# A two-block transformer with a mixture of experts on one core: a reordered router, and expert tiles placed in other buffers

## The chip, the cores and the metric

The kernel runs on one core of a Trainium2 chip. The metric is the device time of one execution, in microseconds, with the weights in HBM at the start and the result written back to HBM.

## The reference, cut to what matters

256 tokens of width 1024 in float32 pass two blocks. The first block (a recurrent and pooling mixer, cross attention, a convolutional feed-forward layer, a conformer convolution, cross attention, the feed-forward layer again) is touched by the change only in which buffers its tiles take. The second block:

```python
def second_block(x, g_mix, w_in, sinks, w_br_dil, w_br_swa, w_out, g_ffn, w_group, b_group,
                 w_router, b_router, w_e_gate, w_e_up, w_e_down, g_final):
    h = rmsnorm(x, g_mix)
    q_d, k_d, v_d, q_s, k_s, v_s, gate_d, gate_s = split_cols(h @ w_in, IN_WIDTHS)
    y_dil = dilated_attention(q_d, k_d, v_d)          # 3 groups of 8 heads
    y_swa = swa_sink_attention(q_s, k_s, v_s, sinks)  # 16 heads, 2 of keys and values
    mixed = sigmoid(gate_d) * (y_dil @ w_br_dil) + sigmoid(gate_s) * (y_swa @ w_br_swa)
    x = x + mixed @ w_out
    x = x + hier_moe(rmsnorm(x, g_ffn), w_group, b_group, w_router, b_router,
                     w_e_gate, w_e_up, w_e_down)
    return rmsnorm(x, g_final)

def hier_moe(h, ...):
    g_logits = h @ w_group + b_group                  # 4 groups, the best one is taken
    e_logits = (h @ w_router + b_router)              # 8 experts of that group, the best two
    ...
    for e in range(32):
        a = silu(h @ w_e_gate[e]) * (h @ w_e_up[e])   # 1024 -> 512
        out = out + gates[:, e:e + 1] * (a @ w_e_down[e])
    return out
```

## The kernel before, in words

Every projection but the experts' is done as three fast matmuls on a split of both sides: ACT makes the high half of a weight tile (`whl`, L219), DVE the low half (L220), and x is held as xth and xtl. Weights come through SP's DMA queue into a ring of three 1 MiB buffers. SP, PE, DVE, ACT and POOL each run their own instructions in program order; a tile framework sets the waits and hands out buffers, and `after` (L325) adds an order without a wait.

**End of the second attention.** `block2_attn` takes its activations from one ring of 16 buffers, `p4`. `proj_rows` multiplies `mixed` by the four w_out tiles; the last two are gone through by quarters of the result (`b` = 0 to 3: token half, column half), and after each quarter the `Norm` class adds the residual to x on DVE (L67), makes xn = x times the gain g_ffn (L73), sums squares on ACT (L84), transposes xn on PE (L354) into PSUM, from where ACT copies it to xnT (L356).

**The router.** `moe` (from L1128) loads the group's and the router's weights as one tile wr of 1024 x 36 (L1155, ACT's queue). `logits` keeps wr as the stationary side, so the result lp lies as 36 x 128; ACT copies it (L1172) and PE transposes it back (L1186). DVE then scales by the token's norm and adds the biases (L1191), picks group and experts (`first_max`, L1120 to 1125), and a matmul with a triangle counts each expert's tokens (L1213). Each expert has 32 slots, four experts (a quad) fill the 128 rows of PE. `gather` (L1238) multiplies xn with a 0/1 matrix and so brings a quad's tokens into slots, 4 chunks of 128 columns at a time.

**The experts.** Eight quads; for each, 8 streams of 1 MiB of gate weights (G), 8 of up weights (U), 8 of down weights (Y, in two halves), 192 MiB in all. One stream is four matmuls (L1325), one for each expert. The tiles live wherever there is room: `wl` counts the streams and takes buffers in a fixed rotation of 22 units of 1 MiB: pairs (2 MiB tiles, L1297) and single homes (L1285). A home in a buffer of the attention (ring, split buffers, xth, xtl, rows, x itself) is issued as soon as SP comes to it and its buffer is free. SP's queue is in order.

x is added to the output accumulators in PSUM by four residual matmuls (L1275), after which x's own buffer is a home. `turn` scales G and U by the gate and transposes them; `scatter` (L1361) brings a half of Y back to the tokens. After the last scatter, ACT squares the four accumulator quarters (L342), DVE and POOL make the norm, and DVE multiplies by it and by the final gain gf (L1408), which was broadcast to all partitions by a DMA.

The rotation before:

```python
pairs = two(r2a[0], "w2") * NR2A + two(r2b, "w3") * NR2B        # 3 and 2 pairs
homes = [lambda s: whole(r2a[1], "w4", s)]
homes += [lambda s: whole(self.ring, "w", s)] * 3
homes += [lambda s: whole(self.spl[0], "whl", s)] * 4
homes += [lambda s: halves([half(self.rows, "row") for _ in range(2)], s)]
homes += [lambda s: whole(self.xtp, "xth", s), lambda s: whole(self.xtp, "xtl", s)]
homes += [lambda s: whole(self.xp, "x", s)]
```

Of the kernel before, what the change touches and what calls it, by code (L numbers as in the profile page):

```python
# [16 lines left out]
P = 128  # L17
# [8 lines left out]
NR2A = 3  # L26
NR2B = 2
# [4 lines left out]
class FM:  # L32


    def __init__(self, k, n, dt, name):
        self.t = [k.b4([P, min(4, n - i), T], dt, f"{name}{i}") for i in range(0, n, 4)]
# [7 lines left out]
class Norm:  # L44
# [57 lines left out]
    def stats(self, t):  # L102
# [3 lines left out]
        nc.vector.scalar_tensor_tensor(r, ss[:, t, 0:1], EPS, ss[:, t, 1:2], op0=OP.add, op1=OP.add)  # L106
# [33 lines left out]

class Kern:
    def __init__(self, ctx, tc, a, out):
        self.tc, self.nc, self.a, self.out = tc, tc.nc, a, out
        self.uid = self.nspl = 0
# [16 lines left out]
    def b4(self, shape, dt=F32, name="b4"):  # L161
        return self.p4.tile(shape, dt, tag="b4", name=self.nm(name))
# [113 lines left out]
    def proj_tm(self, acc, w, ah, al, first):  # L276
# [4 lines left out]
        for k in range(2):  # L281
            for t in range(2):
                sh = ah(k)[:, t * P:(t + 1) * P]
                sl = al(k)[:, t * P:(t + 1) * P]
                st = first and k == 0
                for h in range(2):
                    nc.tensor.matmul(acc[t][h], sh, wh(k)[:, h * 512:(h + 1) * 512], start=st, stop=False)  # L287
                for h in range(2):
                    nc.tensor.matmul(acc[t][h], sh, wl(k)[:, h * 512:(h + 1) * 512], start=False, stop=False)  # L289
                for h in range(2):  # L290
                    nc.tensor.matmul(acc[t][h], sl, wh(k)[:, h * 512:(h + 1) * 512], start=False, stop=False)

    def proj_rows(self, acc, w, ah, al, order, first=True, last=True, norm=None):
# [11 lines left out]
        for b in range(4):  # L305
            t, h = divmod(b, 2)
            ts_ = slice(t * P, (t + 1) * P)
            hs = slice(h * 512, (h + 1) * 512)
            for j, (i, wh, wl) in enumerate(ws):
# [591 lines left out]
    def block2_attn(self, norm):  # L901
# [20 lines left out]
        def qproj(n0, nch, sc0, name):  # L922
            q = FM(self, nch, F32, name)
# [30 lines left out]
        ysh = FM(self, 8, F32R, "ysh")  # L954
        ysl = FM(self, 8, F32R, "ysl")
        qd, kd, vd = [], [], []

        def dil_proj(g):

            q_ = FM(self, 4, F32, "qd")  # L960
            k_ = FM(self, 4, F32, "kd")
            v_ = self.b4([P, 2, 512], F32, "vd")
# [112 lines left out]
        for g in range(3):  # L1075
            steps += dil_proj(g)
        self.reserve(ysh, ysl)
# [5 lines left out]
        ydh = FM(self, 4, F32R, "ydh")  # L1083
        ydl = FM(self, 4, F32R, "ydl")
        gd = FM(self, 8, F32, "gd")
        gs = FM(self, 8, F32, "gs")
# [41 lines left out]
    def moe(self, ctx, m, r2a):  # L1128
# [3 lines left out]
        y2 = pool("y2", 2)  # L1132
# [5 lines left out]

        def t2(shape, name, dt=F32):
            return y2.tile(shape, dt, tag="y2", name=self.nm(name))  # L1140
# [20 lines left out]
        lt = m1([36, 2, P], F32, "lt")  # L1161
# [443 lines left out]
```

## Time and profile before

| | |
|---|---|
| median of 3 runs | 1627.76 us (1627.60 to 1628.19) |
| profiled execution | 1636.39 us |
| its span | 1634.5 us |
| mean granted PE clock | 0.951 of full speed |
| PE, DVE, ACT, POOL busy | 91%, 52%, 41%, 5% |
| HBM read | 393.94 MB, 242 GB/s over the span |

A share of busy time is a mean over a program whose parts differ. Up to about 1150 us PE is busy nine tenths of the time and the DMA engines half of it; from about 1195 us to the end the experts' weights stream, the DMA engines are busy all the time and PE seven tenths. So a change near 1150 to 1200 us is read from windows there and from the queue that issues the weights, not from the shares of the whole. In the timelines a row gives its start, its length, engine, line and operation; in brackets stands the idle time before it and what ended it. Starts are those of the one profiled execution, in us from its span's start.

### The profile page before, as it was taken

To read this page: it belongs to the slowest core of one execution; us is meant where nothing else is said; L and a number is where in the kernel's file an instruction comes from. 1 tells how busy PE (TensorE), PEld (TensorE's weight loads), DVE (VectorE), ACT (ScalarE), POOL (GpSimd) and SP (SyncE) were. 2 spreads that over 40 slices of the span, in tenths; PEclk is the share of its full clock that TensorE was granted. 3 is DMA by queue.
4 is the path that set the end of the run, shared out by engine and by line. 5 is a ranking of instruction groups with operands and counts; after the bars stand their busy time and mean duration, and the time that the engine had idled before them with its cause. 6 is when DMAs were issued, how large, how long until landed. Compare 5 with 4: busy or idle time off the path is not lost. (4 is left out here: it accounts for less than half of the span.)

```text
span 1634.5 us, 23715 instructions
## 1 busy us (share of the span) xinstructions
PE 1479.8 (91%) x9724; PEld 1133.7 (69%) x9724; DVE 851.4 (52%) x1553; ACT 663.8 (41%) x1061; POOL 82.4 (5%) x146
## 2 busy tenths in 40 slices
PE   8999999999989999999999999999998777676665
PEld 7988889999987688999988789789643222221211
DVE  7975677666899566776676765765500000000000
ACT  5764555545676454545554444454311000000001
POOL 0000000000057000100000000000000000000000
PEclk9999999999999999999999999999989878897887
DMA  7555445555643443655545236247999999999996
GB/s 265 193 188 180 143 167 191 185 192 187 218 151 104 161 162 104 219 181 194 186 162 206 99 128 213 78 153 286 356 381 423 421 423 425 424 422 421 425 423 268
DMA packets 52049, 396.58 MB, mean 243 GB/s; under 512 B 5952, under 2 KB 6112, under 8 KB 12256
## 3 DMA queue, kind: packets, MB, share of 16 engines
q1 hardware_dynamic: 49824, 388.80, 62.0%
q0 software_dynamic: 1680, 5.79, 1.1%
q8 instruction: 78, 1.28, 0.3%
q10 hardware_dynamic: 432, 0.41, 0.1%
q14 instruction: 35, 0.29, 0.0%
HBM read 393.94 MB, written 1.05 MB: 242 GB/s over the span
## 5 line engine op out<-in xcount | busy, mean ns | idle before, releaser
L220 DVE TENSOR_TENSOR whl<-w,whl 128x1024 fp32r<-128x1024 f32 (+1 forms) x344 | 404.8, 1184 | 207.3 <-ACT whl L219 206.7
L219 ACT ACTIVATE whl<-w 128x1024 fp32r<-128x1024 f32 (+1 forms) x344 | 345.7, 1020 | 296.3 <-PE pr L270 147.0
L267 PE MATMUL pr<-xth,whl 128*128 128x256 f32 x1472 | 370.0, 283 | 0.0
L268 PE MATMUL pr<-xtl,whl 128*128 128x256 f32 x1472 | 366.8, 281 | 0.0
L267 PEld LDWEIGHTS pr<-xth,whl 128*128 128x128 f32 x1472 | 277.3, 188 | 3.7 <-issue 2.8
L268 PEld LDWEIGHTS pr<-xtl,whl 128*128 128x128 f32 x1472 | 277.2, 188 | 1.9 <-issue 1.1
L270 PE MATMUL pr<-xth,whl 128*128 128x256 f32 x1472 | 236.7, 281 | 1.2 <-DVE whl L220 1.2
L270 PEld LDWEIGHTS pr<-xth,whl 128*128 128x128 f32 x1472 | 200.4, 188 | 2.9 <-issue 1.5
L1387 DVE TENSOR_TENSOR as<-sg,tp 128x512 f32<-128x512 f32 x8 | 5.5, 687 | 241.1 <-ACT GUs L1330 117.2
L1325 PE MATMUL U<-w,xq 128*32 128x512 f32 x512 | 81.0, 719 | 37.4 <-DMA w<-in_w_e_dram 37.3
L1325 PE MATMUL Y<-w,as 128*32 128x512 f32 x512 | 77.4, 737 | 30.4 <-DMA w<-in_w_e_dram 25.4
L1325 PE MATMUL G<-w,xq 128*32 128x512 f32 x512 | 74.0, 671 | 32.5 <-DMA w<-in_w_e_dram 32.5
L1349 DVE COPY sct<-st 128x256 f32<-128x256 f32 x8 | 3.4, 424 | 160.9 <-PE st L1347 160.9
L1325 PEld LDWEIGHTS Y<-w,as 128*32 128x32 f32 x512 | 16.0, 126 | 84.0 <-DMA w<-in_w_e_dram 39.0
L1325 PEld LDWEIGHTS U<-w,xq 128*32 128x32 f32 x512 | 14.4, 119 | 84.0 <-DMA w<-in_w_e_dram 49.7
L1325 PEld LDWEIGHTS G<-w,xq 128*32 128x32 f32 x512 | 13.4, 116 | 83.3 <-DMA w<-in_w_e_dram 62.4
L1395 ACT ACTIVATE ys<-Y,sm 128x512 f32<-128x512 f32 x16 | 11.0, 687 | 130.0 <-PE Y L1325 130.0
L1330 ACT ACTIVATE GUs<-G,sm 128x512 f32<-128x512 f32 x8 | 5.5, 687 | 129.1 <-PE G L1325 129.1
L827 DVE SCALAR_TENSOR_TENSOR cps<-gl,vec,cps 128x252 f32<-128x252 f32 (+18 forms) x144 | 56.1, 468 | 1.7 <-ACT cps L797 1.6
L819 POOL TENSOR_TENSOR cv<-cv,prod 128x470 f32<-128x470 f32 (+9 forms) x40 | 50.4, 1263 | 18.8 <-ACT prod L815 16.3
L287 PE MATMUL pa<-whl,ah 128*128 128x512 f32 x160 | 49.4, 390 | 0.0
L289 PE MATMUL pa<-whl,ah 128*128 128x512 f32 x160 | 49.4, 390 | 0.0
(438 smaller groups left out, 2318.7 us busy)
## 6 DMA issues: line engine op xcount, KB each, us to landing
w<-in_w_e_dram SPq DMA_DIRECT2D x94, 1024.0 KB, 22.5
w<-in_w_e_dram SPq DMA_DIRECT2D x45, 2048.0 KB, 22.3
w<-in_f_w_up_dram SPq DMA_DIRECT2D x48, 1024.0 KB, 4.8
w<-in_w_in_dram SPq DMA_DIRECT2D x25, 1024.0 KB, 4.8
w<-in_f_w_down_dram SPq DMA_DIRECT2D x24, 1024.0 KB, 4.9
w<-in_c_w_pw_dram SPq DMA_DIRECT2D x12, 1024.0 KB, 4.9
w<-in_ab_w_in_dram SPq DMA_DIRECT2D x9, 1024.0 KB, 5.0
w<-in_xa_wk_dram SPq DMA_DIRECT2D x8, 1024.0 KB, 4.9
```

Source lines behind the costliest of these rows:

```text
L219: c = self.last_hi = nc.scalar.activation(h[:, s], src[:, s], AF.Copy)
L220: d = nc.vector.tensor_sub(l[:, s], src[:, s], h[:, s].bitcast(F32))
L267: nc.tensor.matmul(ps[:, j], wh(k)[:, js], xh(k), start=(k == 0), stop=False)
L268: nc.tensor.matmul(ps[:, j], wh(k)[:, js], xl(k), start=False, stop=False)
L270: nc.tensor.matmul(ps[:, j], wl(k)[:, js], xh(k), start=False, stop=(k == kc - 1))
L287: nc.tensor.matmul(acc[t][h], sh, wh(k)[:, h * 512:(h + 1) * 512], start=st, stop=False)
L289: nc.tensor.matmul(acc[t][h], sh, wl(k)[:, h * 512:(h + 1) * 512], start=False, stop=False)
L819: nc.gpsimd.tensor_add(y, y, pd)
L827: nc.vector.scalar_tensor_tensor(y, gl[g][:, j, :T - d], wc(d, 2 * g + j), y, op0=OP.mult, op1=OP.add)
L1325: nc.tensor.matmul(ps[32 * e:32 * e + 32], lh[:, 32 * e:32 * e + 32], w(e), start=st, stop=en)
L1330: nc.scalar.activation(s, src, AF.Copy, scale=gc[:, 1:2])
L1395: nc.scalar.activation(ys, Y, AF.Copy, scale=gc[:, 0:1])
```

## The change

It has five parts.

1. **Buffers.** `p4` becomes two rings, p4b (10) and p4a (6); the smaller one is given up at the end of the dilated attention and its room goes to five pairs (`r2a`, NR2A = 5). `r2b` holds one pair instead of two. The single home w4 and the two halves in `rows` are gone: 6 pairs and 10 homes, again 22 units.
2. **The router.** A class `RouterNorm`: x is transposed, not xn, and the gain g_ffn is multiplied into wr by DVE (from a column gcol, loaded on ACT's queue behind wr). Logits come out with tokens on the partitions, so the copy and the transposes back are gone. The last quarter of the out-projection is done in two pieces of 256 columns, each added to x by itself, and DVE copies the last transposes.
3. **Residuals and the first gather.** Three residual matmuls follow the last logits, the fourth, (1, 1), the fourth G stream of the first quad. The first gather has chunks of 1, 1, 2 and 4, the last two groups ahead of G streams 1 and 2.
4. **Buffers of the experts' loop.** GUs and ys share one (`GUY`), sg and as are one, in the tag `b2`.
5. **The final gain.** No broadcast load. `spread` at the end makes it: DVE puts the gain on a diagonal (dgw), PE multiplies it by ones, ACT copies the row to gf.

The core of the diff (left out: the two rings' tags in the attention, the same edits in the path for experts with more than 32 tokens, and the host's arrangement of the two gains as columns):

```diff
-NR2A = 3
-NR2B = 2
+NR2A = 5
+NR2B = 1
...
+class RouterNorm(Norm):
...
+        if i < 3:
+            nc.vector.tensor_add(x, x, acc[t][h])
+            self.sq(i)
+            self.gain(i)
...
+    def piece(self, p, acc):
+        x = self.k.x[:, 1, 512 + 256 * p:768 + 256 * p]
+        self.k.nc.vector.tensor_add(x, x, acc[1][1][p])
...
+        k.transpose_half(k.x[:, t], t, h, self.th, None)
...
+    def last(self, p):
+        k, nc = self.k, self.k.nc
+        ps = k.psr([P, 2, P], "pt")
+        for c in range(2):
+            o = 512 + 256 * p + c * P
+            nc.tensor.transpose(ps[:, c], k.x[:, 1, o:o + P], k.ident)
+        return nc.vector.tensor_copy(self.ts[1][:, 2 * p:2 * p + 2, P:2 * P], ps)
...
-        lt = m1([36, 2, P], F32, "lt")
+        gcol = m1([P, KC], F32, "gcol")
+        nc.scalar.dma_start(gcol, a["g_ffn_c"])
+        nc.vector.tensor_tensor(wr, wr, gcol[:, :, None].to_broadcast([P, KC, 36]), op=OP.mult)
...
-                nc.tensor.matmul(lps[t], wr[:, k], norm.th(k)[:, t * P:(t + 1) * P], start=(k == 0), stop=(k == KC - 1))
-            if h == 1:
-                nc.scalar.activation(lt[:, t], lps[t], AF.Copy)
+                k += 4 * h
+                self.lp_last = nc.tensor.matmul(lps[t], norm.th(k)[:, t * P:(t + 1) * P], wr[:, k], start=(k == 0), stop=(k == KC - 1))
...
-        norm.then = None
-        norm.b(3)
+        for p in range(2):
+            norm.last(p)
+        norm.sq(3)
         norm.stats(1)
-        logits(3)
+        for p in range(2):
+            logits(3, range(2 * p, 2 * p + 2))
+        acc = self.acc4()
+
+        def residual(t, h):
+            return nc.tensor.matmul(acc[t][h], self.ident, self.x[:, t, h * 512:(h + 1) * 512], start=True, stop=False)
+        for t, h in ((0, 0), (0, 1), (1, 0)):
+            self.after(self.lp_last, residual(t, h))
+        self.after(norm.stt, norm.gain(3))
...
-        pairs = two(r2a[0], "w2") * NR2A + two(r2b, "w3") * NR2B
-        homes = [lambda s: whole(r2a[1], "w4", s)]
-        homes += [lambda s: whole(self.ring, "w", s)] * 3
+        pairs = two(r2a, "w2") * NR2A + two(r2b, "w3") * NR2B
+        homes = [lambda s: whole(self.ring, "w", s)] * 3
         homes += [lambda s: whole(self.spl[0], "whl", s)] * 4
-        homes += [lambda s: halves([half(self.rows, "row") for _ in range(2)], s)]
...
+                if q == 0 and k in (1, 2):
+                    gather(0, 4 * k - 4 or 2, 2 * k, sel)
+                mm = stream(G, x_[:, k], q, k, k == 0, k == KC - 1)
+                if q == 0 and k == 3:
+                    self.after(mm, residual(1, 1))
...
-                ys = t2([P, 512], "ys")
+                ys = m1([P, 512], F32, "ys", "GUY")
...
+        def spread():
+
+            row = []
+            for h in range(2):
+                dg = m1([P, 4, P], F32, "dgw", "GUY" if h else "b2")
+                nc.vector.tensor_tensor(dg, self.ident[:, None, :].to_broadcast([P, 4, P]),
+                                        gc8[:, 4 * h:4 * h + 4, None].to_broadcast([P, 4, P]), op=OP.mult)
+                row.append(self.psr([P, 512], "row"))
+                nc.tensor.matmul(row[h], self.ones, dg.rearrange("p c n -> p (c n)"), start=True, stop=True)
+            gf = big("gf")[:, :D].rearrange("p (h n) -> p h n", h=2)
+            for h in range(2):
+                nc.scalar.activation(gf[:, h], row[h], AF.Copy)
+            return gf
...
-        gf = self.bcast(a["g_final_2"], tile=m1([P, D], F32, "gf"))
```

What it moves, at three places. DVE's queue at the out-projection, as it was (whl: splits of w_out's last two tiles, w; ml: the last split of `mixed`):

```order
L220 TENSOR_TENSOR whl_11292<-w_11287,whl_11292 128x1024
L332 TENSOR_TENSOR ml_11086<-gs_1228_9973,mh_11085 128x512 x2
L220 TENSOR_TENSOR whl_11321<-w_11319,whl_11321 128x1024
L1151 TENSOR_SCALAR tri_11237<-jp 128x128
L220 TENSOR_TENSOR whl_11324<-w_11319,whl_11324 128x1024
L220 TENSOR_TENSOR whl_11329<-w_11327,whl_11329 128x1024
L220 TENSOR_TENSOR whl_11332<-w_11327,whl_11332 128x1024
```

and as it is now:

```order
L269 TENSOR_TENSOR whl_11299<-w_11294,whl_11299 128x1024
L402 TENSOR_TENSOR ml_11087<-gs_1228_9976,mh_11086 128x512
L269 TENSOR_TENSOR whl_11334<-w_11332,whl_11334 128x1024
L1217 TENSOR_SCALAR tri_11235<-jp 128x128
L269 TENSOR_TENSOR whl_11337<-w_11332,whl_11337 128x1024
L1229 TENSOR_TENSOR wr_11239<-wr_11239,gcol_11244 128x288
L269 TENSOR_TENSOR whl_11342<-w_11340,whl_11342 128x1024
L269 TENSOR_TENSOR whl_11345<-w_11340,whl_11345 128x1024
```

The multiply of wr now stands between the splits of the third tile and those of the fourth.

PE's queue from the first gather on, now (ga: the gather; G: gate streams, x8 are two; pa_11476 is residual (1, 1)):

```order
L1313 MATMUL ga_11542<-sel_11535,xn_11360 128x128
L1313 MATMUL ga_11542<-sel_11535,xn_11413 128x128
L1394 MATMUL G_11570<-w_11571,xq_11537 32x512 x4
L1313 MATMUL ga_11577<-sel_11535,xn_11360 128x128
...
L1394 MATMUL G_11570<-w_11571,xq_11537 32x512 x4
L1313 MATMUL ga_11587<-sel_11535,xn_11360 128x128
...
L1394 MATMUL G_11570<-w_11597,xq_11537 32x512 x8
L1257 MATMUL pa_11476<-x,ident 128x512
```

Before, all 32 gather matmuls stood ahead of the first G stream, and the four residuals among the logits. On SP, x's home (the last single of the rotation) now follows the fourth residual, and the reloads of the pairs follow it:

```order
L1356 DMA w_11756<-in_w_e_dram 128x2048
L1356 DMA w_11762<-in_w_e_dram 128x2048
L1368 DMA w_11770<-in_w_e_dram 128x4096
L1368 DMA w_11783<-in_w_e_dram 128x4096
L1368 DMA w_11795<-in_w_e_dram 128x4096
```

w_11762 is x's home, w_11770 the first reload of a pair; the order of the kinds is that of before, what x waits for is not.

ACT's queue at the end, before and then now:

```order
L1395 ACTIVATE ys_13127<-Y_13104,sm_13013 128x512
L342 ACTIVATE junk_13162,sm_13163<-pa_11552 128x512
L1395 ACTIVATE ys_13156<-Y_13129,sm_13013 128x512
L342 ACTIVATE junk_13162,sm_13163<-pa_11553 128x512
L342 ACTIVATE junk_13169,sm_13170<-pa_11554 128x512
L342 ACTIVATE junk_13169,sm_13170<-pa_11555 128x512
```

```order
L1469 ACTIVATE ys_13111<-Y_13090,sm_13002 128x512
L1469 ACTIVATE ys_13140<-Y_13113,sm_13002 128x512
L1489 ACTIVATE gf_13154<-row_13148 128x512
L412 ACTIVATE junk_13157,sm_13158<-pa_11473 128x512
L1489 ACTIVATE gf_13154<-row_13152 128x512
L412 ACTIVATE junk_13157,sm_13158<-pa_11474 128x512
L412 ACTIVATE junk_13164,sm_13165<-pa_11475 128x512
L412 ACTIVATE junk_13164,sm_13165<-pa_11476 128x512
```

The two copies of gf stand among the squares, behind both halves of Y.

## Rows read from the trace of the kernel before

**Rows 1.** Windows of 50 us: engines' busy us, PEclk, DMA share, GB/s; first, last of eight.
```profile
1200.00:1250.00 50.00, 46.58 (x362) 19.28 (x358) 2.81 (x9) 8.99 (x13) 0.00 (x0) 0.97 1.01 423
...
1550.00:1600.00 50.00, 32.51 (x186) 7.74 (x190) 1.11 (x6) 2.66 (x4) 0.00 (x0) 0.84 1.01 424
```

**Rows 2.** The same columns in windows of 1 us around the restart of the weights.
```profile
1190.00:1191.00 1.00, 1.00 (x7) 1.00 (x6) 0.00 (x0) 0.00 (x0) 0.00 (x0) 0.52 0.67 279
...
1193.00:1194.00 1.00, 1.00 (x16) 0.29 (x12) 0.00 (x0) 0.00 (x0) 0.00 (x0) 1.00 0.00 0
...
1197.00:1198.00 1.00, 1.00 (x12) 0.26 (x8) 0.88 (x5) 0.00 (x0) 0.00 (x0) 1.00 1.03 442
```

**Rows 3.** Timeline of SP's queue: start, us, engine, line, operation (last: the restart).
```profile
1150.33 0.86 SPq L1297 DMA_DIRECT2D w<-in_w_e_dram  x2
...
1175.64 5.54 SPq L1285 DMA_DIRECT2D w<-in_w_e_dram  x3
1193.57 0.33 SPq L1297 DMA_DIRECT2D w<-in_w_e_dram  x1
```

**Rows 4.** Timeline of the tail: start, us, engine, line, operation [idle before <-releaser].
```profile
1619.47 1.06 PE L1325 MATMUL Y<-w,as 128*32 128x512 f32 x8 [1.43 <-DMA w<-in_w_e_dram]
1620.61 0.69 ACT L1395 ACTIVATE ys<-Y,sm 128x512 f32<-128x512 f32 x1 [6.32 <-PE Y L1325]
...
1621.35 3.51 PE L1361 MATMUL pa<-ys,sct 128*128 128x512 f32 x4 [0.81 <-ACT ys L1395]
...
1623.46 0.60 ACT L342 ACTIVATE junk<-pa 128x512 bf16<-128x512 f32 x1 [2.17 <-PE pa L1361]
```

**Rows 5.** Timeline from the out-projection's last matmul to the router's scores.
```profile
1173.38 0.40 PE L317 MATMUL pa<-whl,ml 128*128 128x512 f32 x1
...
1173.82 0.69 DVE L67 TENSOR_TENSOR x<-x,pa 128x512 f32<-128x512 f32 x1 [3.29 <-PE pa L317]
...
1175.29 0.16 DVE L106 SCALAR_TENSOR_TENSOR rn<-ssn 128x1 f32<-128x1 f32 x1
...
1175.53 0.55 POOL L108 TENSOR_TENSOR rn<-rn,neghalf 128x1 f32<-128x1 f32 x1 [8.80 <-DVE rn L106]
...
1175.66 0.60 PE L354 MATMUL pt<-ident,xn 128*128 128x128 f32 x4
...
1177.43 1.06 PE L1170 MATMUL lp<-xnT,wr 128*36 128x128 f32 x8
...
1179.66 1.13 PE L1275 MATMUL pa<-x,ident 128*128 128x512 f32 x2
1179.83 0.41 DVE L1191 SCALAR_TENSOR_TENSOR Le<-lp,rn,rb 128x32 f32<-128x32 f32 x2 [4.38 <-PE lp L1186]
```

**Rows 6.** Timeline of the first gather and of the first G streams.
```profile
1183.63 0.31 PE L1213 MATMUL pp<-sel,tri 128*128 128x32 bf16 x2 [2.85 <-DVE sel L1205]
...
1185.02 6.64 PE L1238 MATMUL ga<-sel,xn 128*128 128x128 f32 x32 [0.88 <-DVE cmi L1219]
...
1191.59 3.64 PE L1325 MATMUL G<-w,xq 128*32 128x512 f32 x32
```

**Rows 7.** The page's groups: a DVE copy of 128x256.
```profile
L1349 DVE COPY sct<-st 128x256 f32<-128x256 f32 x8 | 3.4, 424 | 160.9 <-PE st L1347 160.9
```

**Rows 8.** Timeline around wr's issue and the last split of the last w_out tile.
```profile
1151.17 0.33 ACTq L1155 DMA_DIRECT2D wr<-in_w_rt_dram  x1
...
1159.63 1.22 DVE L220 TENSOR_TENSOR whl<-w,whl 128x1024 fp32r<-128x1024 f32 x1 [1.58 <-ACT whl L219]
...
1160.91 0.50 PE L316 MATMUL pa<-whl,mh 128*128 128x512 f32 x1
```

**Rows 9.** DMA issues: KB each, us from issue to landing.
```profile
wr<-in_w_rt_dram ACTq DMA_DIRECT2D x1, 144.0 KB, 12.8
```

**Rows 10.** The tile dgw, at the program's start: duration ns min/median/max.
```profile
L427 PE MATMUL row<-dgw,ones x4: 1061/1061/1192, 4.8 to 7.5; 128*128 128x512 f32 x4
L425 DVE TENSOR_TENSOR dgw<-ident,sm x2: 683/688/693, 4.0 to 4.6; 128x512 f32<-128x512 f32 x2
```

More of the change, by code (lines that the diff above doesn't have):

```diff
@@ L32, with __init__ @@
 class FM:
-    def __init__(self, k, n, dt, name):
-        self.t = [k.b4([P, min(4, n - i), T], dt, f"{name}{i}") for i in range(0, n, 4)]
+    def __init__(self, k, n, dt, name, own=None):
+        self.t = [k.b4([P, min(4, n - i), T], dt, f"{name}{i}", own) for i in range(0, n, 4)]
     def __call__(self, c, n=1):
@@ L308, in proj_rows @@
             hs = slice(h * 512, (h + 1) * 512)
+            if b == 3 and isinstance(norm, RouterNorm):
+                norm.a(3)
+                for p in range(2):
+                    o = acc[1][1][p]
+                    cs = slice(512 + 256 * p, 768 + 256 * p)
+                    for j, (i, wh, wl) in enumerate(ws):
+                        for k in range(2):
+                            if (p, j, k) == (0, 1, 0):
+                                norm.b(2)
+                            sh, sl = ah(2 * i + k)[:, ts_], al(2 * i + k)[:, ts_]
+                            nc.tensor.matmul(o, sh, wh(k)[:, cs], start=False, stop=False)
+                            nc.tensor.matmul(o, sh, wl(k)[:, cs], start=False, stop=False)
+                            nc.tensor.matmul(o, sl, wh(k)[:, cs], start=False, stop=(j == 1 and k == 1))
+                    norm.piece(p, acc)
+                break
             for j, (i, wh, wl) in enumerate(ws):
@@ L1174, in moe @@
         nX, nT = iter(range(2)), iter(range(2))
-        norm = Norm(self, a["g_ffn_2"], then=logits,
-                    tiles=(lambda: m1([P, D], F32, "xn", f"xn{next(nX)}"), lambda: m1([P, 4, T], F32, "xnT", f"xs{next(nT)}")))
-        self.proj_rows(self.acc4(), lambda i: a["w_out_2"][i], *m, range(4), norm=norm)
+        norm = RouterNorm(self, a["g_ffn_2"], then=logits,
+                          tiles=(lambda: m1([P, D], F32, "xn", f"xn{next(nX)}"), lambda: m1([P, 4, T], F32, "xnT", f"xs{next(nT)}")))
@@ L1269, in moe @@
         nc.vector.tensor_mul(gov, gov, gat)
-        acc = self.acc4()
-        for t in range(2):
-            for h in range(2):
-                nc.tensor.matmul(acc[t][h], self.ident, self.x[:, t, h * 512:(h + 1) * 512], start=True, stop=False)
         self.wn = -1
```

136 lines of the change are left out of this document (85 added, 51 removed).

## Prediction

> **What bounds the kernel now.** I read the windows of 50 us first. In each of the eight from 1200 to 1600 us the 16 DMA engines are fully used at 422 to 424 GB/s [rows 1]. So the last quarter of the run is a transfer: 1 MiB takes 1.0486 MB / 423 GB/s = 2.48 us, and the end is the moment at which the weights' stream restarts, plus the MiB still to come x 2.48, plus a tail after the last weights. The next view is in windows of 1 us: before the restart the DMA goes quiet, because every buffer is full [rows 2], for some 3 us up to 1194. The timeline of SP's queue says why: 22 units of 1 MiB are issued up to 1181 us, and the next only at 1193.57, when the first pair of expert tiles has been read [rows 3]. Of 192 MiB 170 are then left: 1194 + 170 x 2.48 = 1615.6, and the last piece lets PE go on at 1619.47 [rows 4]. The timelines of the router [rows 5] and of the first gather [rows 6] say what sets 1193.57: the out-projection's last matmul ends at 1173.38 + 0.40, the scores start on DVE at 1179.83, the gather at 1185.02, the G streams at 1191.59, of which the first two free the pair. The timeline of the tail has the rest [rows 4].
>
> The sums are made against this profiled execution (1636.39 us, span 1634.5). The median of the runs, 1627.76, is 8.6 us lower; I carry differences over.
>
> **The pairs placed earlier: 0.** Five pairs (10 MiB) are sent during the attention where three pairs, a single and half of another were (7.5 MiB). The total stays at 22 units (6 pairs and 10 single homes for 5 pairs and 12), and all but one (next part) are full before the restart in either kernel. The four split buffers, xth and xtl still come free only as the out-projection ends: 6 x 2.48 = 15 us from about 1175.5, so they are full at about 1190.5, ahead of the restart. What was brought earlier is repaid as idle DMA. Ends: 0, and a gain of 2.5 MiB x 2.48 = 6.2 us.
>
> **The home in x moves behind the restart: +2.5.** Before, x was free when the fourth residual matmul ended at 1180.79 [rows 5], and its home was issued as the last of the 22 [rows 3]. Now residual (1,1) stands behind the fourth G stream, and x's home stands in SP's queue ahead of the first reload of a pair. At the restart 21 units are in and 171 MiB are left: +2.48 us.
>
> **When the restart comes: +0.7.** Four pieces, made against 1193.57.
> - *Shorter router chain, -3.1.* Before, 1173.78 to 1179.83, 6.05 us: an add of 0.69, the row product, four transposes, an ACT copy, logits behind a residual matmul, a copy and transposes back [rows 5]. After, on DVE and PE: an add of 256 columns (0.42, the price of a DVE copy of that shape [rows 7]), two transposes (half of 0.60 [rows 5]), two copies of 0.42, the STT 0.16, then POOL's power 0.55 with 0.24 ahead of it and some 0.25 behind, the four narrow logit matmuls and the row product of 0.69 beside it: 0.42 + 0.3 + 0.84 + 0.16 + 1.04 = 2.76, with two hops of 0.1 about 2.95. The 5.2 us from scores to gather stay.
> - *Narrower logits inside the out-projection, -0.4.* In 12 matmuls 36 columns move instead of 128 (8 took 1.06 before [rows 5]).
> - *The gain folded into wr, +2.1, the least certain term.* The multiply stands on DVE between the splits of the third and of the fourth w_out tile and waits for wr. wr took 12.8 us to land [rows 9] when it was issued at 1151.17 [rows 8], beside some 5 MiB (two pairs at 1150.33 [rows 3], one single just ahead). Now it is issued about 1.5 us later beside some 3 MiB. Behind the multiply are two splits of 1.22; before, the second ended at 1160.85, and PE stood waiting for it at 1160.91 [rows 8]. So PE is held for t_w + 0.5 + 2 x 1.25 - 1160.9 = t_w - 1157.9, t_w being the landing. By what is queued beside it, 12.8 x 3/5 = 7.7 and t_w = 1160.4; with 2 MiB, 5.1 and 1157.8. I take 1160: +2.1. Ends: 0, and +7.6 with 12.8 us as before. What the reordered mixer and the attention gain or lose upstream, up to 1 us, lies under this wait.
> - *What releases the restart, +2.1.* Gather and G streams hold the same passes, interleaved: 10.2 us from 1185.02 to the end of the fourth stream [rows 6] (32 matmuls take 3.64, so eight streams of four). Residual (1,1) adds 0.56 (1.13 for two [rows 5]). x's home is thus issued 10.7 us after the gather's start, where the first reload was issued 1193.57 - 1185.02 = 8.55 after it. The pairs' reloads stand behind it on SP, though the first pair is free some 2 us sooner.
>
> Sum: -3.1 - 0.4 + 2.1 + 2.1 = +0.7. Ends: -1.5 without the wait for wr, +6.2 with the longest.
>
> The Trainium skill (DMA: Bandwidth & Descriptors, Queues, rings and completion order) says that a DMA engine takes turns between queues, packet by packet. By that wr, on ACT's queue, would not stand behind SP's backlog, and this sum would be -1.4 instead of +0.7; the 12.8 us of wr's own row speaks against it.
>
> **The tail, +4.3.** Before, the final gain lay ready as a broadcast load. After the last Y matmul (end 1620.53) come ys, the scatter, and the square of tile 0's second half at 1623.46 [rows 4]; tile 0's first half had been squared long before. Now the gain row is made there, and ACT's order is ys, gf, square, gf, square, square, square. The first gf waits for a ones-matmul that stands behind the last scatter matmul on PE: 1621.35 + 3.51 = 1624.86 [rows 4], + 1.06 [rows 10] = 1625.9; gf to 1626.5; the square of the first half (0.60 and 0.2 for its sum) to 1627.3; the second gf (its diagonal, 0.69 on DVE [rows 10], waits for the buffer that the last scatter reads, so its matmul ends near 1626.7) to 1627.9. The second square starts there instead of at 1623.46: +4.3 or a little more, all on the path. Ends: +3.7 with PE at full clock, +5.6 with all of it at half.
>
> **Transfer rate: 0.** A broadcast of 0.5 MiB and 16 half-size loads go. Windows with and without half-size loads lie between 422 and 424 GB/s: at most 1.7 us gained.
>
> Total: 0 + 2.5 + 0.7 + 4.3 = **+7.5 us**: 1643.9 for a profiled execution, 1635.3 for the median; I say 1635.0.
>
> **Rivals.**
> - *wr as late as before.* It lands 12.8 us after its issue and PE is held 7.6 us instead of 2.1: 1640.5. For: its row; against: less is queued beside it. 0.12.
> - *The clock stays up in the gather.* The 32 passes took 6.64 us at a granted clock near 0.50 [rows 2, 6], after PE had idled 2.85 us for the select; now residuals fill a part of that idle time. At full clock 2.6 us come back: 1632.4. Against: over 2 us of idling remain. 0.12.
> - *The pairs pay.* If the fills still run when the stream restarts, the 2.5 MiB sent earlier count in full, -6.2: 1628.8. For: the DMA is full from 1157 to 1190; against: the quiet before the restart [rows 2]. 0.09.
> - *Faster, by the rate.* Place: the stream from 1194 on. With the half-size loads gone every transfer is of 1 or 2 MiB. 171 MiB are 179.3 MB, 423.9 us at 423 GB/s; to repay 7.5 us it must run at 430.6, so that is the point from which it decides. At 440, just under the best microsecond [rows 2], it takes 407.5, net -8.9: 1618.9. Against: none of eight windows is over 424 [rows 1]. 0.06.
> - That the change does not do what it says is no rival here: the order on each queue shows every part of it.
>
> Beside the last but one: the same page (Bandwidth, Where 436 GB/s comes from) puts a ceiling of 435 GB/s on the ports; by it that rival would end at 1623.6. The rows stand 3% below it.
>
> **Numbers.** The forecast, 1631.5 to 1638.5, has 0.61. The range 1629.5 to 1640.5 takes in the clock, part of "the pairs pay" and most of a late wr, and leaves out 2 in 10 at most. A measurement of this kernel tells about 0.2%, 3.3 us, from no change: faster is below 1624.5, the same up to 1631.0. Faster: the rate, and half as much for a gain unseen here, 0.09. Same: the pairs, and several low ends together (wr early, clock up, tail 3.7), 0.12. Slower: the rest, 0.79.
>
> **What would show it.** In the profile after: a quiet stretch of the DMA of 2 to 4 us before the restart; as its first issue a single of 1 MiB right behind residual (1,1), near 1194; scores that start 2.9 us after the out-projection's last matmul; a wait of DVE ahead of the multiply of wr and one of PE, 1 to 3 us, for the fourth tile's splits; 422 to 424 GB/s in all windows after; the first square behind the last scatter 7 us after the last Y matmul's end, not 2.9. It is wrong if the restart comes before 1191, if the DMA never goes quiet, if the multiply of wr waits for nothing, or if gf stands ready before the last Y.

## The result, and the profile after

| | median of its runs | profiled execution | its span |
|---|---|---|---|
| before | 1628.05 us (6 runs, 1627.6 to 1635.03) | 1636.39 us | 1634.5 us |
| changed | 1646.08 us (6 runs, 1639.57 to 1647.08) | 1646.81 us | 1645.0 us |

The ratio is 1.0080 with an interval of [1.0056, 1.0103] (the two medians alone would give 1.0111): slower by about 0.8%. Forecast were 1635.0 us and a range up to 1640.5; the sign was right, the size was not.

Executions of one and the same kernel differ by 5 to 11 us here, so below, medians and ratios with many runs stand for times, and profiles are compared from the out-projection's first matmul on, behind three places at which PE's granted clock falls in some profiles and not in others (last section). In the two profiles of this section it falls at all three, and up to that first matmul they differ by 0.6 us, so most of their difference of 10.5 us is that of the change. The three times shown ahead of the prediction, 1627.60 to 1628.19 us, lie at the low end of what the kernel before does: over the later runs it has 1626.7 to 1638.2 us and a median of some 1635.5, and 1646.08 is 10.6 above that. Differences between kernels below are differences of medians, each good to some 3 us.

The anchors are the first matmul on mh and, at the other end, the first multiply of the last output piece. Of the kernel before, in its timeline (start, us, engine, line, operation, [idle before <-releaser]):

```profile
1147.13 0.63 PE L287 MATMUL pa<-whl,mh 128*128 128x512 f32 x2
...
1627.14 1.41 DVE L1408 SCALAR_TENSOR_TENSOR fin<-pa,sm,gf 128x512 f32<-128x512 f32 x2 [0.66 <-POOL sm L345]
```

The timeline of the changed kernel through the out-projection, the router, the first gather and the restart; it answers to [rows 3, 5, 6, 8]:

```profile
1147.77 0.63 PE L342 MATMUL pa<-whl,mh 128*128 128x512 f32 x2
...
1153.16 0.35 ACTq L1221 DMA_DIRECT2D wr<-in_w_rt_dram  x1
...
1153.55 0.46 ACTq L1228 DMA_DIRECT2D gcol<-in_g_ffn_c_dram  x1
...
1165.64 0.46 DVE L1229 TENSOR_TENSOR wr<-wr,gcol 128x288 f32<-128x288 f32 x1 [9.28 <-DMA gcol<-in_g_ffn_c_dram]
1166.02 2.35 DVE L269 TENSOR_TENSOR whl<-w,whl 128x1024 fp32r<-128x1024 f32 x2
...
1167.29 0.80 PE L386 MATMUL pa<-whl,mh 128*128 128x512 f32 x1 [6.52 <-DVE whl L269]
...
1181.93 0.28 PE L376 MATMUL pa<-whl,ml 128*128 128x256 f32 x1
...
1184.97 0.45 DVE L1266 SCALAR_TENSOR_TENSOR Le<-lp,rn,rb 128x32 f32<-128x32 f32 x2 [0.24 <-issue]
...
1190.21 1.13 PE L1313 MATMUL ga<-sel,xn 128*128 128x128 f32 x8 [0.88 <-DVE cmi L1294]
...
1199.43 0.33 SPq L1356 DMA_DIRECT2D w<-in_w_e_dram  x1
...
1199.80 6.24 SPq L1368 DMA_DIRECT2D w<-in_w_e_dram  x5
```

The reader is to see one long gap in the middle. DVE stood 9.28 us ahead of the multiply of wr, and the releaser is not wr: it is gcol, the 4 KB of the router's gain as a column, which the multiply reads as well. Behind it stood the last splits, and behind these PE, 6.52 us. The view of DMA issues (KB each, us from issue to landing) has both transfers, beside [rows 9]:

```profile
wr<-in_w_rt_dram ACTq DMA_DIRECT2D x1, 144.0 KB, 9.1
...
gcol<-in_g_ffn_c_dram ACTq DMA_DIRECT2D x1, 4.0 KB, 12.0
...
gc<-in_g_final_c_dram ACTq DMA_DIRECT2D x1, 4.0 KB, 14.0
```

wr was in at 1153.16 + 9.1 = 1162.3, the column at 1153.55 + 12.0 = 1165.55, where the multiply starts. The third load of that queue, gc (the final gain, issued at 1154.07), was in at 1168.1, another 2.5 us later: here each load landed behind the one ahead of it on its queue, however small it was. The windows (span, then busy us of PE, PEld, DVE, ACT, POOL, the granted clock, DMA share, GB/s) show what came with it:

```profile
1157.00:1163.00 6.00, 3.77 (x20) 2.85 (x18) 0.00 (x0) 1.50 (x2) 0.00 (x0) 1.00 0.99 309
1163.00:1173.00 10.00, 5.71 (x16) 4.52 (x17) 4.11 (x5) 0.72 (x2) 0.00 (x0) 0.66 0.70 266
1174.00:1177.00 3.00, 3.00 (x21) 2.64 (x20) 1.18 (x3) 1.81 (x4) 0.56 (x1) 1.00 0.00 0
1198.00:1199.00 1.00, 1.00 (x6) 0.44 (x3) 0.00 (x0) 0.00 (x0) 0.00 (x0) 1.00 0.12 49
...
1550.00:1600.00 50.00, 34.19 (x194) 7.77 (x186) 1.79 (x7) 3.35 (x5) 0.00 (x0) 0.79 1.01 424
```

After the idle time PE came back at a mean granted clock of 0.66 (between its two levels of 1.2 and 2.4 GHz). The DMA is quiet twice: for some 9 us from 1173 to 1182, while the held out-projection keeps the split buffers, and again just ahead of the restart. The last window is that of [rows 1], at the same 424 GB/s. The timeline of the tail, beside [rows 4]:

```profile
1626.80 1.06 PE L1394 MATMUL Y<-w,sg 128*32 128x512 f32 x8 [1.42 <-DMA w<-in_w_e_dram]
...
1628.73 1.98 PE L1431 MATMUL pa<-ys,sct 128*128 128x512 f32 x4 [0.87 <-ACT ys L1469]
...
1630.55 2.14 PE L1486 MATMUL row<-dgw,ones 128*128 128x512 f32 x4
...
1631.61 0.60 ACT L1489 ACTIVATE gf<-row 128x512 f32<-128x512 f32 x1 [2.93 <-PE row L1486]
...
1633.22 0.59 ACT L412 ACTIVATE junk<-pa 128x512 bf16<-128x512 f32 x1
...
1636.96 1.41 DVE L1500 SCALAR_TENSOR_TENSOR fin<-pa,sm,gf 128x512 f32<-128x512 f32 x2 [0.66 <-POOL sm L415]
```

Taken apart, stage by stage, us:

| stage | before | changed | difference |
|---|---|---|---|
| upstream, to the first matmul on mh | 1147.13 | 1147.77 | +0.6 |
| out-projection, to its last matmul's end | 26.65 | 34.44 | +7.8 |
| to the first scores | 6.05 | 2.76 | -3.3 |
| to the first gather | 5.19 | 5.24 | +0.1 |
| to the restart's first issue | 8.55 | 9.22 | +0.7 |
| to the last Y matmul | 425.90 | 427.37 | +1.5 |
| to the first multiply of the last piece | 7.67 | 10.16 | +2.5 |
| rest | 7.36 | 8.04 | +0.7 |

The sum is 10.6 (10.5 before rounding). Most of it is one stage, the out-projection. ("Last Y matmul" is the start of the last row of Y matmuls.)

### The profile page after: what moved, and what is told of

Its sections match the earlier page's. It is cut to its first block, busy times and chain, and to the rows that moved or that the text cites. A ratio compares the mean times of both kernels' runs of the same rounds, so it can differ in the third digit from the quotient of the medians.

```text
span 1645.0 us, 23746 instructions
## 1 busy us (share of the span) xinstructions
PE 1473.6 (90%) x9750; PEld 1132.1 (69%) x9750; DVE 852.1 (52%) x1559; ACT 659.2 (40%) x1058; POOL 83.5 (5%) x145
## 5 line engine op out<-in xcount | busy, mean ns | idle before, releaser
L1461 DVE TENSOR_TENSOR sg<-sg,tp 128x512 f32<-128x512 f32 x8 | 5.5, 688 | 239.8 <-ACT GUs L1400 152.0
L1394 PE MATMUL Y<-w,sg 128*32 128x512 f32 x512 | 76.5, 723 | 35.7 <-DMA w<-in_w_e_dram 30.7
L1394 PEld LDWEIGHTS Y<-w,sg 128*32 128x32 f32 x512 | 15.2, 122 | 88.9 <-DMA w<-in_w_e_dram 47.5
L1394 PEld LDWEIGHTS U<-w,xq 128*32 128x32 f32 x512 | 13.4, 119 | 87.2 <-DMA w<-in_w_e_dram 55.1
```

Source lines behind the costliest of these rows:

```text
L1394: mm = nc.tensor.matmul(ps[32 * e:32 * e + 32], lh[:, 32 * e:32 * e + 32], w(e), start=st, stop=en)
```

## The experiments

The theory after reading the traces, A: three added waits cost the time (the multiply of wr ahead of the last splits, the final gain made in the tail, and residual (1,1) with x's home behind it), and each can be undone alone. Its main rival, B: the loss lies elsewhere, in the order of the loads or in buffers that come free late, and undoing these moves little. The first four kernels ran together, beside 35 runs of the kernel before (median 1635.67 us).

**The multiply behind the last split.** Only its place on DVE changes.

```diff
         ws = [(i, *self.split(self.wload(w(i), 2, D))) for i in order[n:]]
+        if isinstance(norm, RouterNorm):
+            self.after(self.last_lo, norm.mul)
```

> The changed kernel with one order added: the multiply of wr by the gain stands on DVE behind the splits of the last w_out tile instead of ahead of them. Theory A (the multiply's wait for the gain column, landed at 1165.6, holds two splits, and PE's idling then brings half clock): PE's wait of 6.5 us at 1167 and the slow stretch behind it vanish, the out-projection's last matmul ends near 1174 instead of 1182.2, x's home is issued near 1191 instead of 1199.4, and the time falls by about 8 us. Rival B (the fills of the buffers, not the router, set the restart, so that an earlier router only waits for transfers): the fills end near 1190 and the time falls by 2 us or less. Rival C (PE is held elsewhere in the out-projection): no change.

Measured: 1639.71 us, ratio 1.0024 [1.0003, 1.0045], 6.4 us below the changed kernel. Its timeline and windows:

```profile
1161.48 0.46 DVE L1231 TENSOR_TENSOR wr<-wr,gcol 128x288 f32<-128x288 f32 x1 [3.91 <-DMA gcol<-in_g_ffn_c_dram]
```

```profile
1163.00:1173.00 10.00, 9.71 (x75) 8.86 (x73) 4.41 (x10) 4.59 (x12) 0.56 (x1) 1.00 0.37 133
```

The multiply still waits 3.91 us for the column, but now only the first add to x stands behind it (PE waits 1.7 us for that add), and PE holds its full clock in the window, where the changed kernel had 0.66. (This profile's out-projection begins 3.9 us earlier, at 1143.84.) The out-projection takes 27.59 us instead of 34.44. So one placement, with nothing else touched, carries most of the loss: 6.9 us of its stage, 6.4 of the median.

**The final gain loaded, as before.** It is broadcast by a DMA again instead of made by matmuls in the tail.

```diff
-            gf = spread()
...
+        row = self.bcast(a["g_final_2"]).rearrange("p (h n) -> p h n", h=2)
+        finish(lambda t, h: acc[t][h], row)
```

> The changed kernel with the final gain broadcast by a DMA into one of the two row buffers, as in the kernel before, instead of being made by DVE, PE and ACT behind the last scatter. Theory A: the first square behind the last scatter starts 2.9 us after the last Y matmul's end instead of 5.4, and the time falls by 2.5 us. Rival B (the tail's length is set by the clock of the scatter and by the chain of norms, not by the gain): under 1 us.

Measured: 1643.44 us, 1.0052 [1.0035, 1.0070], -2.6 us. Its tail:

```profile
1625.30 1.06 PE L1394 MATMUL Y<-w,sg 128*32 128x512 f32 x8 [1.42 <-DMA w<-in_w_e_dram]
...
1627.08 0.59 ACT L412 ACTIVATE junk<-pa 128x512 bf16<-128x512 f32 x1
...
1632.14 1.41 DVE L1499 SCALAR_TENSOR_TENSOR fin<-pa,sm,row 128x512 f32<-128x512 f32 x2 [0.66 <-POOL sm L415]
```

The first square follows ys at once, and the stretch from the last Y to the last piece is 6.84 us instead of 10.16. The making of the gain lay on the path, as the prediction had it; its price is taken up below.

**Residual (1,1) with the other three.**

```diff
-        for t, h in ((0, 0), (0, 1), (1, 0)):
+        for t, h in ((0, 0), (0, 1), (1, 0), (1, 1)):
...
-                if q == 0 and k == 3:
-                    self.after(mm, residual(1, 1))
```

> The changed kernel with residual (1,1) beside the other three, ahead of the select, instead of behind the fourth G stream, so that x's home is issued some 10 us earlier and no longer holds the reloads of the pairs. Theory A: the DMA's quiet stretch near 1198 to 1201 goes, x's home joins the fills, the first reload is issued near 1194.5, and the time falls by 2 to 3 us. Rival B (the reloads are held by something else, or the earlier residual holds the select or the gather on PE): no change, or 0.5 us slower.

Measured: 1642.95 us, 1.0046 [1.0028, 1.0065], -3.1 us. SP's queue and one window:

```profile
1187.30 0.33 SPq L1356 DMA_DIRECT2D w<-in_w_e_dram  x1
...
1193.37 10.61 SPq L1368 DMA_DIRECT2D w<-in_w_e_dram  x5
```

```profile
1198.00:1199.00 1.00, 1.00 (x11) 0.51 (x14) 0.63 (x4) 0.00 (x0) 0.00 (x0) 1.00 1.06 442
```

x's home goes out 6 us ahead of the first reload of a pair instead of with it, and the quiet microsecond of the changed kernel at 1198 is full. From the first gather to the last Y this profile is 3.3 us shorter. It doesn't show in its total, since the column landed later here (14.0 us after its issue) and PE waited 8.8 us for the splits.

**All three.** The edits of the three together.

> The three edits together: the multiply behind the splits, the final gain loaded, residual (1,1) early. Theory A (three terms that add): -8.4 -2.5 -2.5, so 13 us below the changed kernel and about level with the kernel before or 2 to 4 us faster, with the DMA never quiet between the out-projection and the end. Rival B (the fills become the bound): the gains overlap and 8 us or less are left, so the kernel stays slower than before by 5 us or more.

Measured: 1633.71 us, 0.9987 [0.9970, 1.0004]: 12.4 us below the changed kernel, where the three alone add up to 6.4 + 2.6 + 3.1 = 12.1, and level with the kernel before. Medians that are good to 3 us can't show that the three don't overlap; the stages of the profiles can, taken as in the table above:

| kernel | out-projection | first gather to last Y | last Y to last piece | first matmul on mh to the span's end |
|---|---|---|---|---|
| before | 26.65 | 434.45 | 7.67 | 487.4 |
| changed | 34.44 | 436.59 | 10.16 | 497.2 |
| multiply behind the split | 27.59 | 438.12 | 12.92 | 494.0 |
| gain loaded | 33.94 | 436.45 | 6.84 | 492.8 |
| residual early | 36.66 | 433.28 | 11.81 | 497.1 |
| all three | 27.77 | 433.45 | 6.84 | 483.8 |

Each edit shortens its own stage, by 6.9, 3.3 and 3.3 us (13.5 together), and all three take 13.4 off the whole. So A holds, and they add. What else moves in the single rows is the column's landing and PE's clock: with the multiply moved the gather ran at a mean clock of 0.72 and the tail in part at half clock. The shorter router chain (-3.3) should be left as a gain; the point is 2.1 us below before, with an interval from -4.9 to +0.7, so whether it arrives can't be told. The windows show that the DMA stands still for longer than the 3 us or so of before [rows 2], some 6 us:

```profile
1162.00:1165.00 3.00, 3.00 (x21) 2.63 (x20) 0.58 (x2) 1.05 (x3) 0.56 (x1) 1.00 0.34 139
1165.00:1168.00 3.00, 3.00 (x28) 2.95 (x28) 1.45 (x3) 1.32 (x3) 0.00 (x0) 1.00 0.00 0
1168.00:1171.00 3.00, 2.70 (x26) 2.46 (x24) 1.42 (x4) 1.23 (x3) 0.00 (x0) 1.00 0.58 147
```

Every buffer that is free is full; the split buffers, and the tiles that hold mh and ml, come free only as the out-projection ends.

The next three ran beside 29 runs of the kernel before (1635.46 us).

**The column at the program's start**, on the changed kernel: was it the column or wr that the multiply waited for?

```diff
+        self.gcol = self.cst([P, KC], F32, "gcol")
+        nc.scalar.dma_start(self.gcol, a["g_ffn_c"])
...
-        gcol = m1([P, KC], F32, "gcol")
-        nc.scalar.dma_start(gcol, a["g_ffn_c"])
+        gcol = self.gcol
```

> The changed kernel with the gain column (128 x 8, 4 KB) loaded at the program's start instead of behind wr at 1153.6; the multiply stays ahead of the splits and then waits for wr alone. Theory A (the 4 KB column, 12.0 us from issue to landing, ended the wait; wr itself, 9.1 us, landed near 1162.3): the multiply starts near 1162.3, counted against an out-projection that begins at 1147.8, PE's wait falls from 6.5 to about 3.2 us, and the time by 3 to 5 us. Rival B (both loads wait for the same backlog, so that wr alone lands as late): the wait stays over 5 us and the time within 1.5 us.

Measured: 1640.90 us, 1.0047 [1.0029, 1.0065], -5.2 us. The column takes 3.3 us there. The timeline:

```profile
1162.73 0.46 DVE L1230 TENSOR_TENSOR wr<-wr,gcol 128x288 f32<-128x288 f32 x1 [5.93 <-DMA wr<-in_w_rt_dram]
...
1164.37 0.50 PE L386 MATMUL pa<-whl,mh 128*128 128x512 f32 x1 [2.70 <-DVE whl L269]
```

The multiply now waits for wr, and PE's wait falls from 6.52 to 2.70 us. So the column, not wr, ended the wait. (The early tile also shifts all others in SBUF by 32 bytes, which has an effect of its own, below.)

**Split buffers free sooner**, on the kernel with all three undone: the third w_out tile goes into all four quarters first, then the fourth, so that two of the four split buffers come free sooner.

```diff
+            for q in qs:
+                for k in range(2):
+                    part(0, k, *q)
+            for b, q in enumerate(qs):
+                for k in range(2):
...
+                    part(1, k, *q)
```

> The kernel with the three edits, and the last two w_out tiles gone through one after the other: all quarters take the third tile first, then the fourth, so that two of the four split buffers come free some 5 us before the out-projection ends. Theory A (the end is set by the buffers that are free while the DMA stands idle, some 6.5 us between 1162.7 and 1169.5 in the profile of the three edits): two more units go out in that time, the idle stretch falls to about 1.5 us, and the kernel is 4 to 5 us faster than with the three edits. Rival B (from the restart on the router's chain decides): no change, or 1 us slower where the norm's steps now stand closer together.

Measured: 1625.81 us, 0.9946 [0.9929, 0.9964]. This version beats both kernels, by 9.7 and 20.3 us of median. The window that was empty above:

```profile
1165.00:1168.00 3.00, 3.00 (x23) 2.68 (x22) 1.37 (x4) 1.73 (x4) 0.56 (x1) 1.00 1.02 426
```

SP's queue has the next home of all three undone, and then the next two of this kernel:

```profile
1168.27 0.33 SPq L1359 DMA_DIRECT2D w<-in_w_e_dram  x1
```

```profile
1161.65 0.80 SPq L1388 DMA_DIRECT2D w<-in_w_e_dram  x2
```

Counted from the first matmul on mh (1141.49 and 1145.02) that is 26.8 and 16.6 us, 10 us earlier. The idle DMA was worth time: the intervals of the two kernels do not touch, and from the first matmul on mh to the last Y the profiles have 469.2 and 464.3 us, 4.9 less. How the other 3 us between the medians came about is not settled.

Nor are the 4.9 us the freed buffers' alone. The new order also gives PE work while DVE waits for the column: the wait of 1.9 us that all three undone still have is gone, and the out-projection takes 25.57 us instead of 27.77. Where the column is out of the way on both sides (two kernels further down, with medians of 1629.92 and 1628.45), the same reordering takes 2.2 us off the stretch to the last Y, 463.2 to 460.9, and 1.5 off the median, which the intervals can't tell from nothing.

**Two of the five pairs late**, on the kernel with all three undone: pairs 4 and 5 are issued behind the last w_out load.

```diff
-                self.after(self.anchor, nc.sync.dma_start(t, a["w_e_2"][q, i // 2]))
+                dd = nc.sync.dma_start(t, a["w_e_2"][q, i // 2])
+                self.after(self.last_wout if self.wn in (6, 8) else self.anchor, dd)
```

> The kernel with the three edits, but the fourth and fifth pair are issued behind the last w_out tile's load instead of during the attention. Theory A (placing the pairs early is worth nothing, since the DMA catches up in its idle time before the out-projection ends): the idle stretch of 6.5 us shrinks by what is sent later, and the time stays within 1 us of the three edits. Rival B (the pairs pay): 2 to 6 us slower.

Measured: 1637.18 us, 1.0023 [1.0003, 1.0043], 3.5 us over all three undone. That looks as if the early place paid. The views of DMA issues, and of PE's waits from 1139 to 1176 us (engine, line, awaited: us, times, longest), say otherwise:

```profile
wr<-in_w_rt_dram ACTq DMA_DIRECT2D x1, 144.0 KB, 12.4
...
gcol<-in_g_ffn_c_dram ACTq DMA_DIRECT2D x1, 4.0 KB, 16.1
```

```profile
PE pt L427 <- DVE x L154: 4.6, 1, 4.6
```

With two more pairs in flight the column lands after 16.1 us, and PE waits 4.6 us (1.9 with all three undone alone) for the add behind the multiply. The pairs may have cost nothing themselves; that needed a kernel without the column. The next two, beside 23 runs of the kernel before (1635.51), are a pair for this:

**Both with the column early.** One is two pairs late, the three edits and the column at the start; the other leaves the pairs in their early place.

> The three edits with two pairs sent late, as in the run before, and the gain column loaded at the program's start. That run was 3.5 us slower than the three edits alone, while its idle stretch of the DMA was the same 6 us. Theory A (the pairs' place is worth nothing to the transfer; sent late they only held up the gain column, 16.1 us to landing instead of 12.0, and with it DVE, PE's transposes and PE's clock): without the column in the way the loss goes, and the kernel is within 1 us of the next run, which has the pairs early. Rival B (the pairs' early place pays by itself): it stays 3 us or more slower than the next run.

> The three edits and the gain column loaded at the program's start, the pairs early. PE's wait of 1.9 us for the first transposes, which stood behind the multiply on DVE, goes. Theory A: 1 to 2 us faster than the three edits (1632.5 in the mean of 12 runs, 1633.7 in the median). Rival B (the wait is hidden): no change.

Measured: 1630.34 us, 0.9979 [0.9965, 0.9993], and 1629.92 us, 0.9980 [0.9964, 0.9995]. They are equal within their intervals of some 2 us: no worth of the pairs' early place shows, and the 3.5 us above came through the column's landing.

**The best version with the column early**, and two that ask why that gained nothing. The second gives the column 64 bytes instead of 32, the third leaves the column where it was and puts an unused tile of 32 bytes ahead of all others.

```diff
+        self.gcol = self.cst([P, 2 * KC], F32, "gcol")[:, :KC]
```

```diff
+        pad = self.cst([P, KC], F32, "pad")
+        nc.gpsimd.memset(pad, 0.0)
```

> The version with two split buffers freed early, and the gain column loaded at the program's start. There PE waited for nothing in the out-projection and the DMA was busy without a break, so the column's wait on DVE (4.0 us) was covered. Theory A (the transfer alone sets the end from there on): no change against that version (1625.3 in the mean of 12 runs), within 1 us. Rival B (the wait still reached the router through DVE): 1 to 2 us faster.

> The run before with the early gain column kept in 64 bytes per partition instead of 32. In every run with the 32-byte column the out-projections' matmuls of 512 columns took 394 to 395 ns, in all others 389, and the last out-projection began 3 us later or so; the column's tile sits ahead of all others in SBUF and moves their addresses by 32 bytes. Theory A (the address of the operands does it): 389 ns again, the last out-projection's start 2 to 4 us earlier, and 1622 to 1624 us in the mean. Rival B (the early load itself, or an extra wait, does it): 394 ns again and 1627 to 1628.

> The version with two split buffers freed early, unchanged but for an unused tile of 32 bytes per partition ahead of all others in SBUF (one small memset on POOL). In the four runs with the 32-byte column there the weights' stream ran at 427 to 429 GB/s instead of 423 to 425 and the matmuls of 512 columns took 394 to 395 ns instead of 389; with 64 bytes the stream was at 424 again. Theory A (the operands' addresses do both): 428 GB/s and 394 ns here too, the stream about 4 us shorter, the PE-bound part before it about 3 to 5 us longer, the time as before, 1624 to 1628 us. Rival B (the early load does it): 424 GB/s and 389 ns.

Measured: 1628.45 us, 0.9962 [0.9947, 0.9977]; 1627.57 us, 0.9954 [0.9936, 0.9972]; 1625.47 us, 0.9951 [0.9936, 0.9966]. None is clear of the version with the split buffers alone (0.9946). The matmul groups (ns min/median/max, first and last start) and a window of that version:

```profile
L342 PE MATMUL pa<-whl,ah x160: 387/389/402, 255.0 to 817.8; 128*128 128x512 f32 x160
```

```profile
1300.00:1600.00 300.00, 203.62 (x1230) 60.54 (x1230) 10.30 (x39) 21.50 (x33) 0.00 (x0) 0.84 1.01 424
```

And with the unused 32 bytes ahead:

```profile
L342 PE MATMUL pa<-whl,ah x160: 389/394/403, 253.4 to 820.2; 128*128 128x512 f32 x160
```

```profile
1300.00:1600.00 300.00, 206.43 (x1234) 62.29 (x1238) 10.31 (x39) 21.51 (x33) 0.00 (x0) 0.82 1.01 428
```

The shift of addresses alone makes the stream faster and the matmuls slower, and the time stays. The 64-byte column took the stream back to 424 GB/s, but its matmuls stayed at a median of 394 ns: that half was not as expected and is left open.

## Why the prediction was wrong, point by point

**The step that failed is "the gain folded into wr, +2.1".** It named itself the least certain term, and its arithmetic holds: "PE is held for t_w - 1157.9". With the landing that the multiply really waited for, 1165.55, it gives 7.65, and the out-projection became 7.8 longer. That the two are so close is in part luck: PE's wait was 6.52, since it went on behind the first of the two splits, and the rest is the clock behind the wait. What was wrong is the transfer: the step counted wr and left out the 4 KB of the column, which the same instruction reads and which is issued behind wr on the same queue. wr itself landed at 1162.3, 2.3 later than taken; the column came 3.3 us behind that. The kernel with the column early shows the share of it (PE's wait 2.70 instead of 6.52), and the multiply behind the splits shows the whole (-6.9 in the stage, -6.4 in the median). A second piece was missed: after the wait PE ran at a mean clock of 0.66. The step had charged the wait alone.

The end of the step's own bounds, +7.6, was about right, and the rival "wr as late as before" has the price and the place, with another transfer as its cause.

**The page weighed against it.** The column of 4 KB took 12.0 us beside the backlog and 3.3 us at the program's start, and 16.1 us with two more pairs in flight. The Trainium skill (DMA: Bandwidth & Descriptors, Queues, rings and completion order) says that a DMA engine takes turns between queues packet by packet. As the prediction read that rule it would have given a short landing; the rows disagree with that reading: in the eight kernels that issue the column behind wr it lands 2.4 to 4.6 us behind wr, and wr itself takes 8.2 to 12.4 us.

**Terms that held.** The shorter router chain: -3.1 forecast, -3.3 measured. The pairs placed early: 0 forecast, 0 within some 2 us by the pair of kernels with the column early. The transfer rate: 0 forecast, 424 GB/s in the last window of either. The home in x and the residual: the first issue at the restart is a single, right behind residual (1,1), as described; forecast were +2.5 for the home and +2.1 for what releases the restart, 4.6 together; the profiles show +1.5 and +0.7, and undoing that part gives 3.1. Of the missing 2.4, most is a rival that came true, with a price of 2.6: the clock stayed at 1.00 through the gather, where [rows 2] had 0.52. The kernel with the multiply moved bears it out: there the gather ran at 0.72, and its home was issued 10.8 us after the gather's start, near the 10.7 that the prediction had; in the changed kernel it was 9.2. First the changed kernel, then that one:

```profile
1182.00:1198.00 16.00, 13.53 (x102) 8.19 (x101) 7.84 (x47) 3.96 (x9) 0.93 (x1) 1.00 0.97 391
```

```profile
1179.00:1185.00 6.00, 5.58 (x32) 3.04 (x32) 1.40 (x9) 0.94 (x3) 0.00 (x0) 0.72 1.02 422
```

```profile
1179.42 1.13 PE L1316 MATMUL ga<-sel,xn 128*128 128x128 f32 x8 [0.88 <-DVE cmi L1297]
...
1190.26 0.33 SPq L1359 DMA_DIRECT2D w<-in_w_e_dram  x1
```

One price in that sum was misread. In these rows one float32 matmul of the program stands as two: the x2 row of 1.13 in [rows 5] is one residual and not two, so residual (1,1) adds 1.13, not 0.56 (the changed kernel's took 1.12), and 32 rows of G are the four streams that the sum goes by, not eight.

```profile
1198.23 1.12 PE L1257 MATMUL pa<-x,ident 128*128 128x512 f32 x2
```

**The tail** came out under its low end of +3.7: +4.3 forecast, +2.5 in the stages, -2.6 when undone (-3.3 in the stretch of its profile). The scatter took 1.98 us, at full clock, where the sum took the 3.51 of [rows 4]. That is the execution that was profiled: in two other profiles with the same tail the scatter took longer, and the stretch became 12.92 and 11.81 us, 5.3 and 4.1 more than before. The multiply moved, then the residual early:

```profile
1620.34 3.78 PE L1434 MATMUL pa<-ys,sct 128*128 128x512 f32 x4 [0.87 <-ACT ys L1472]
```

```profile
1624.26 3.35 PE L1431 MATMUL pa<-ys,sct 128*128 128x512 f32 x4 [0.87 <-ACT ys L1467]
```

**The sum against its own time** was 1643.9 for a profiled execution, and that came to 1646.81: 2.9 off, made of 6.1 too little for the out-projection (7.8 where -0.4 and +2.1 stood), 2.4 too much for the home and the restart, 1.8 too much for the tail, 0.2 too little taken off for the chain, and 1.3 upstream and at the very end that no term had. The forecast of the median was off by 11.1, and the other 8 are no mechanism of this change: it carried the change over to the three times shown before, which lay at the lower end of what the kernel before does. For the same reason the 0.2% that the prediction gave to a measurement was too small.

**Not foreseen at all:** that the DMA would stand still in the out-projection already, for want of split buffers that come free; the prediction had them full in time, ahead of the restart.

## What to carry to other kernels

Before an instruction that joins two loads is placed ahead of work that others wait for, cost the last of all its operands to land, the small one included: 4 KB issued behind 144 KB, beside an expert backlog, came later than the large one. If a gain on a chain does not arrive at the end, look for idle DMA and ask which buffers it waits for; here an order that frees two buffers some 10 us earlier, and gives PE work during a wait, took the ratio from 0.9987 to 0.9946. An experiment that moves one load can move another's landing: measure it again with that other one taken out.

## What the runs showed of the hardware that was not expected

Two things. A shift of all tiles by 32 bytes raised the weights' stream from 424 to 428 GB/s and took the median of the 512-column matmuls from 389 to 394 ns; over 425 us of stream the first is worth an estimated 4 us, and the time stays within its interval. All kernels with the small tile ahead of the others have the faster stream, 428 GB/s from 1300 to 1600 us; all without it, and the one with 64 bytes, have 424 or 425. Why is open.

And the clock falls upstream of the out-projection in some profiles and not in others. The same window of the changed kernel and of the one with all three undone (clock in the third column from the end):

```profile
540.00:555.00 15.00, 15.00 (x54) 9.26 (x53) 5.79 (x11) 6.03 (x8) 1.89 (x2) 0.77 0.37 128
```

```profile
540.00:555.00 15.00, 15.00 (x64) 9.17 (x64) 8.16 (x15) 7.66 (x12) 1.69 (x2) 1.00 0.45 153
```

PE is busy for all of the window in both, with 54 matmuls begun at 0.77 and 64 at 1.00, and the changed kernel's PE waits for nothing from 505 us to the window's end. What it did before the clock fell at 547 us were, from 543 us on, matmuls of a single column (L917, 128x1) among those of 512; the other kernel had the same ones and kept its clock. At the two other places, near 490 and 890 us, PE had waited (4.1 and 1.3 us in both kernels), and again the clock falls further in the changed kernel. Among the kernels without the small tile the first matmul on mh begins between 1139.3 us (only the first place fell) and 1147.8 us (all three did), so these places can make some 8 us, an estimate from these profiles. That they make the spread between executions of one kernel is likely, but not shown, as each kernel has one profile. What decides it is open.
